# A decoder layer on one core: the operands of all large products laid to the same place modulo 512 bytes

## The chip, the core and the metric

The kernel runs on one core of one Trainium2 chip. The core has five engines that run side by side: TensorE (PE, matrix products; its loading of the stationary operand is shown apart as PEld), VectorE (DVE), ScalarE (ACT), GpSimd (POOL) and SyncE (SP), whose queue issues most of the DMA transfers. SBUF is the working memory, 128 partitions wide; a tile is a stretch of bytes at the same address in each partition. PSUM takes the results of the products. The metric is the device time of one execution in microseconds (us), lower being better.

## The reference

One layer works on 256 positions of width 2048 (all sizes float32):

```
h    = RMSNorm(x);  qkv = h @ W_in
8 heads: stick-breaking attention;  8 heads: rotary + dilated sliding-window attention
x    = x + RMSNorm(concat(RMSNorm per head) @ W_out)
h    = RMSNorm(x);  u = causal depthwise conv (width 3) of h @ W_up   (W_up: 2048 x 11008)
f    = gelu(gate half of u) * (value half of u)
x    = x + RMSNorm(f @ W_down)                                       (W_down: 5504 x 2048)
```

Nearly all of the arithmetic is in the four products with W_in, W_out, W_up and W_down.

## The kernel before

**Precision.** Each large product is made of three: both operands are split into a high part (rounded to the float32r format that TensorE takes) and a low remainder, and high x high, low x high and high x low are summed in PSUM. ScalarE makes the high part of a weight (`high`, line 85), VectorE the low part (`low`, line 90).

**Weights.** They are loaded from DRAM in pieces of 128 x 1024 float32 into `raw` (5 buffers), and their parts go to `wh` and `wl` (4 buffers each), all in the pool `wpool`. `ahead` loads two chunks ahead and splits one chunk ahead of use.

**The large products**, each a stationary operand of 128 x 128 that is loaded anew for each matmul, and a moving operand that streams past it:

- `mm_stationary` (lines 96 to 104): results `mmqk` (queries and keys) and `mmu` (up projection). The weight is stationary, the activation `hT2` moves. In groups of 16: eight matmuls of 512 columns (line 101, the high part of the weight against high and low of the activation at once) and eight of 256 (line 104, low against high). `mm_stationary_late` (line 110) does the first two chunks of the up projection in another order, with 256 columns each.
- `mm_moving` (lines 132 to 149): results `mmv` (values) and `mmo` (output projection). The activation is stationary, `hT2` for `mmv` and the pair `mix` for `mmo`; the weight moves, 512 columns (lines 143, 144, 147).
- `Down.multiply` (lines 621 to 623): result `p`, the down projection; `yt` and `yp` (the activation) are stationary, the weight moves, 512 columns, and 256 for the last 24.

Small products of the attention (lines 340 to 419) stand between those of the first part. One of them is the pair of lines 387 and 388, 384 columns, in which `sph` and `spl` move past `tri`.

**Order.** The chunks of all the products run one after the other in one list; at each chunk the kernel issues its loads, splits and matmuls, and then lets the attention heads advance by a step. The order within an engine is the order of the program, fixed by hand in the passages where `pinned` is set. No wait is written by hand: the framework puts in those that the data and the buffers need.

**Where the tiles lie.** A pool lays its tiles one behind the other, in the order in which they first appear, each rounded up to 32 bytes; the pools follow each other. `cpool` begins at byte 384 of a partition. A float32 tile row of 128 takes 512 bytes, and every slice that the products take of a tile begins a multiple of 512 bytes from the tile's start. What decides the place modulo 512 are thus the tiles whose size is no multiple of 512: `par` (1568 bytes), `rstd1` (8, rounded to 32), `gpre` (64) and the pool `small` (2496 in all).

`along_rows` (line 305) turns a value per position into a row that all partitions hold: VectorE scales the identity by the values (line 310) and TensorE multiplies it by a tile of ones (line 311). It is used twice.

Of the kernel before, what the change touches and what calls it, by code (L numbers as in the profile page):

```python
# [9 lines left out]
F32 = mybir.dt.float32  # L10
F32R = mybir.dt.float32r
BF16 = mybir.dt.bfloat16
AF = mybir.ActivationFunctionType
ALU = mybir.AluOpType
PSUM = bass.MemoryType.PSUM

P = 128
D = 2048
S = 256
KT = D // P  # L20
# [31 lines left out]
def layer_kernel(ctx: ExitStack, tc: tile.TileContext, a, out: bass.AP):  # L52
    nc = tc.nc
    V, A, T, G = nc.vector, nc.scalar, nc.tensor, nc.gpsimd

    cpool = ctx.enter_context(tc.tile_pool(name="cpool", bufs=1))
    wpool = ctx.enter_context(tc.tile_pool(name="wpool", bufs=3))
    small = ctx.enter_context(tc.tile_pool(name="small", bufs=4))
# [139 lines left out]


    A.preload_act_table_set("natural_log_exp_and_others")  # L200
    par = cpool.tile([P, P_END], F32, name="par")
    ident = cpool.tile([P, P], F32, name="ident")
    hT2 = cpool.tile([P, KT, 2, S], F32R, tag="hT", name="hT")
    hT = [hT2[:, :, i, :] for i in range(2)]

    phA = tc.tile_pool(name="phA", bufs=2)
    apool = phA.__enter__()
    cst = apool.tile([P, C_END - P], F32, name="cst", bufs=1)
    gpre = apool.tile([P, KT], F32, name="gpre", bufs=1)
    x1 = apool.tile([P, 2, D], F32, name="x1", bufs=1)  # L210
    x1_kept = nc.dram_tensor("x1_kept", (S, D), F32, kind="Internal").ap()

# [77 lines left out]
    between[10] = (cst, a["cst"][:, 0:C_ID])  # L290
    between[11] = (par, a["par"])

    negones = apool.tile([P, P], F32, name="negones", bufs=1)
    G.memset(negones, -1.0)
    ones = cpool.tile([P, P], F32, name="ones")
    G.memset(ones, 1.0)
    tri = apool.tile([P, P], F32R, name="tri", bufs=1)
    idb = apool.tile([P, P], BF16, name="idb", bufs=1)
    mskb = apool.tile([P, P], BF16, name="mskb", bufs=1)
    rB = apool.tile([P, 2, S], F32, name="rB", bufs=1)  # L300
    cosR = apool.tile([P, 2, S], F32, name="cosR", bufs=1)
    sinR = apool.tile([P, 2, S], F32, name="sinR", bufs=1)
    rstd1 = cpool.tile([P, 2], F32, name="rstd1")

    def along_rows(r, name):

        ps = ps_at.tile([P, S], F32, tag="at", name=name)
        for t in range(2):
            dg = small.tile([P, P], F32, tag="diag", name="diag", bufs=1)
            V.tensor_scalar(dg, ident, r[t], None, op0=ALU.mult)  # L310
            T.matmul(ps[:, t * P:(t + 1) * P], ones, dg, start=True, stop=True)
        return ps

    def first_norm():

        V.tensor_copy(tri, cst[:, C_TRI:C_TRI + P])
        G.tensor_copy(idb, ident)
        G.tensor_copy(mskb, cst[:, C_MSK:C_MSK + P])
        ss = small.tile([P, 2], F32, tag="ssx", name="ssx", bufs=1)
        for t in range(2):  # L320
            A.activation(gbc, x1[:, t, :], AF.Square, accum_out=ss[:, t:t + 1])
        v0 = small.tile([P, 2], F32, tag="vx", name="vx", bufs=1)
        V.tensor_scalar(v0, ss, 1.0 / D, EPS, op0=ALU.mult, op1=ALU.add)
        V.tensor_copy(rstd1, rstd_of(v0, 2))
        rps = along_rows((rstd1[:, 0:1], rstd1[:, 1:2]), "rps")
        V.tensor_scalar(rB[:, 0, :], rps, SCALE, None, op0=ALU.mult)
        V.tensor_copy(rB[:, 1, :], rps)
        for s in range(2):
            V.tensor_tensor(cosR[:, s, :], cst[:, C_COS:C_COS + S], rB[:, s, :], op=ALU.mult)
            V.tensor_tensor(sinR[:, s, :], cst[:, C_SIN:C_SIN + S], rB[:, s, :], op=ALU.mult)  # L330
# [129 lines left out]
    def second_norm():  # L460

        rs = [sq.newton(*sq.mean(t)) for t in range(2)]
        r2B = cpool.tile([P, S], F32, name="r2B")
        V.tensor_scalar(r2B, along_rows(rs, "r2ps"), -0.5, None, op0=ALU.mult)
        return r2B
# [273 lines left out]
    for i, (kind, p, s, _, w) in enumerate(chunks):  # L739
        parts = ahead(i, 0 if (kind, p, s) == ("out", 3, 3) else SPLITS)  # L740
        if kind == "v":
            if s == 0:
                pool, tag = (ps_at, "at") if p == 1 else (ps_mm, "mm")
# [26 lines left out]
        elif kind == "qk":  # L770
            ps = ps_mm.tile([P, 2, S], F32, tag="mm", name="mmqk")
# [8 lines left out]
        elif kind == "out":  # L780
# [14 lines left out]
            else:  # L795
                pinned[0] = True
                up0 = []
                r = [None, None]
# [97 lines left out]
        else:  # L896
            ps = ps_mm.tile([P, 2, S], F32, tag="mm", name="mmu")
# [96 lines left out]
```

## Time and profile before

| what | value |
|---|---|
| median of 3 runs | 1117.11 us (1116.38 to 1117.14) |
| the profiled execution, its time | 1117.05 us |
| its span, first to last instruction | 1115.3 us |
| granted TensorE clock | 0.998 |
| TensorE busy / weight loads | 1103.5 us / 942.1 us |
| VectorE / ScalarE / GpSimd busy | 879.4 / 661.3 / 5.7 us |
| matmuls | 5855 |
| moved by DMA | 257.79 MB, mean 231 GB/s |

The profile is one execution, recorded by the hardware. A line number such as L101 is that of the kernel; `mmu<-hT,wl` names the tile written and the tiles read. In a row of groups stand the number of instructions after the x, then the busy time in us and the mean duration of one in ns, then the idle time before them. In a row by tile stand the shortest, median and longest duration in ns, and when the first and the last began. In a row of the stretches stand the bounds, the length, and then the busy time of PE, PEld, DVE, ACT and POOL with the number of their instructions, the granted clock, the DMA share and GB/s. A matmul's recorded duration reaches beyond the start of the next one, since matmuls are pipelined.

### The profile page before, as it was taken

To read this page: it belongs to the slowest core of one execution; us is meant where nothing else is said; L and a number is where in the kernel's file an instruction comes from. 1 tells how busy PE (TensorE), PEld (TensorE's weight loads), DVE (VectorE), ACT (ScalarE), POOL (GpSimd) and SP (SyncE) were. 2 spreads that over 40 slices of the span, in tenths; PEclk is the share of its full clock that TensorE was granted. 3 is DMA by queue.
4 is the path that set the end of the run, shared out by engine and by line. 5 is a ranking of instruction groups with operands and counts; after the bars stand their busy time and mean duration, and the time that the engine had idled before them with its cause. 6 is when DMAs were issued, how large, how long until landed. Compare 5 with 4: busy or idle time off the path is not lost.

```text
span 1115.3 us, 16308 instructions
## 1 busy us (share of the span) xinstructions
PE 1103.5 (99%) x5855; PEld 942.1 (84%) x5855; DVE 879.4 (79%) x1371; ACT 661.3 (59%) x1046; POOL 5.7 (1%) x13
## 2 busy tenths in 40 slices
PE   9999999999999999999999999999999999999997
PEld 6888888888888888888888888888888888888885
DVE  6577776777776589878888878888878898889887
ACT  6656665655654476655555555555555566666564
POOL 0000000000000000000000000000000000000001
PEclk9999999999999999999999999999999999999999
DMA  9977777877879856555555555555555577767775
GB/s 322 360 261 270 254 252 273 295 255 274 274 258 321 274 199 212 190 189 190 187 189 184 189 186 186 186 188 188 189 188 188 174 250 242 251 217 252 240 244 208
DMA packets 75393, 257.79 MB, mean 231 GB/s; under 512 B 8496, under 2 KB 9520, under 8 KB 74544
## 3 DMA queue, kind: packets, MB, share of 16 engines
q1 hardware_dynamic: 74880, 256.22, 68.9%
q8 instruction: 46, 0.75, 0.3%
q10 hardware_dynamic: 432, 0.53, 0.1%
q14 instruction: 35, 0.29, 0.1%
HBM read 238.89 MB, written 17.83 MB: 230 GB/s over the span
## 4 chain that ended last, share of the span: by engine, by line
PE 98%; DMA 0%; DVE 0%; ACT 0%; issue 0%; SPq 0%; DVEq 0%; ACTq 0%
PE mmu L101 28%; PE mmu L104 14%; PE mmqk L101 11%; PE p L621 7%; PE p L623 7%; PE p L622 6%; PE mmqk L104 5%; PE mmv L144 3%; PE mmv L147 3%; PE mmv L143 3%; PE mmo L143 3%; PE mmo L144 3%; PE mmo L147 3%; PE mmu L110 1%; DMA raw<-in_w_v 0%; PE po L341 0%
## 5 line engine op out<-in xcount | busy, mean ns | idle before, releaser
L88 ACT CAST wh<-raw 128x1024 fp32r<-128x1024 f32 (+1 forms) x408 | 414.8, 1024 | 355.9 <-PE mmu L101 190.1
L93 DVE TENSOR_TENSOR wl<-raw,wh 128x1024 fp32r<-128x1024 f32 (+1 forms) x408 | 482.4, 1189 | 165.4 <-ACT wh L88 160.7
L101 PE MATMUL mmu<-hT,wh 128*128 128x512 f32 x1344 | 340.5, 395 | 0.0
L101 PEld LDWEIGHTS mmu<-hT,wh 128*128 128x128 f32 x1344 | 240.8, 188 | 44.6
L104 PEld LDWEIGHTS mmu<-hT,wl 128*128 128x128 f32 x1344 | 184.1, 188 | 15.3
L104 PE MATMUL mmu<-hT,wl 128*128 128x256 f32 x1344 | 187.3, 281 | 0.0
L101 PE MATMUL mmqk<-hT,wh 128*128 128x512 f32 x512 | 133.0, 401 | 0.0
L101 PEld LDWEIGHTS mmqk<-hT,wh 128*128 128x128 f32 x512 | 92.0, 188 | 17.2
L104 PEld LDWEIGHTS mmqk<-hT,wl 128*128 128x128 f32 x512 | 69.9, 188 | 5.8
L621 PE MATMUL p<-wh,yp 128*128 128x512 f32 x182 | 71.7, 394 | 0.0
L623 PE MATMUL p<-wl,yp 128*128 128x512 f32 x182 | 71.5, 393 | 0.0
L104 PE MATMUL mmqk<-hT,wl 128*128 128x256 f32 x512 | 71.1, 281 | 0.0
L622 PE MATMUL p<-wh,yp 128*128 128x512 f32 x182 | 70.7, 388 | 0.0
L621 PE MATMUL p<-wh,yt 128*128 128x512 f32 (+1 forms) x140 | 54.2, 387 | 0.0
L623 PE MATMUL p<-wl,yt 128*128 128x512 f32 (+1 forms) x140 | 53.8, 386 | 0.0
L622 PE MATMUL p<-wh,yt 128*128 128x512 f32 (+1 forms) x140 | 53.5, 382 | 0.0
L494 ACT ACTIVATE cv<-u,par 128x256 f32<-128x256 f32 x86 | 51.5, 599 | 2.5 <-DVE u L492 2.3
L143 PE MATMUL mmv<-wh,hT 128*128 128x512 f32 x128 | 51.4, 403 | 0.3 <-ACT hT L225 0.3
L144 PE MATMUL mmv<-wh,hT 128*128 128x512 f32 x128 | 50.7, 396 | 0.5 <-DVE hT L272 0.2
L143 PE MATMUL mmo<-wh,mix 128*128 128x512 f32 x128 | 50.4, 394 | 0.0
L88 ACT CAST wh<-room 128x1024 fp32r<-128x1024 f32 x26 | 27.3, 1048 | 38.7 <-PE p L622 36.4
L144 PE MATMUL mmo<-wh,mix 128*128 128x512 f32 x128 | 49.9, 390 | 0.0
(179 smaller groups left out, 1221.8 us busy)
## 6 DMA issues: line engine op xcount, KB each, us to landing
raw<-in_w_up SPq DMA_DIRECT2D x172, 512.0 KB, 4.3
raw<-in_w_qk SPq DMA_DIRECT2D x64, 512.0 KB, 4.9
raw<-in_w_dn SPq DMA_DIRECT2D x60, 512.0 KB, 4.5
raw<-in_w_o SPq DMA_DIRECT2D x32, 512.0 KB, 5.1
raw<-in_w_v SPq DMA_DIRECT2D x28, 512.0 KB, 5.2
t<-in_w_dn SPq DMA_DIRECT2D x26, 512.0 KB, 5.6
t_kept<-t SPq DMA_DIRECT2D x26, 512.0 KB, 3.9
raw<-t_kept SPq DMA_DIRECT2D x26, 512.0 KB, 4.4
```

The lines of the kernel that those rows point to most:

```text
L88: pin(A.copy(wh, raw))
L93: pin(V.tensor_tensor(wl, raw, wh.bitcast(F32), op=ALU.subtract))
L101: T.matmul(ps, wh[:, j * P:(j + 1) * P], h[:, k, :, :], start=(k == 0), stop=False, skip_group_check=True)
L104: T.matmul(ps[:, 0, :], wl[:, j * P:(j + 1) * P], h[:, k, 0, :], start=False, stop=(k == KT - 1), skip_group_check=True)
L110: T.matmul(ps[:, part, :], parts[k // 8][low][:, k % 8 * P:(k % 8 + 1) * P], h[:, k, part, :], skip_group_check=True, **kw)
L143: T.matmul(ps[t], hi[:, k, tc_], ws, start=(first and i == 0 and j == 0), stop=False)
L144: T.matmul(ps[t], lo[:, k, tc_], ws, start=False, stop=False)
L147: T.matmul(ps[t], hi[:, k, tc_], wl[:, j * 512:(j + 1) * 512], start=False, stop=(last and i == len(parts) - 1 and j == n - 1))
L494: A.activation(cv, u, AF.Identity, scale=cw(2), bias=par[:, P_CB + f:P_CB + f + 1])
L621: T.matmul(ps, yh, wh[:, cs], start=key not in self.begun, stop=False)
L622: T.matmul(ps, yl, wh[:, cs], start=False, stop=False)
L623: T.matmul(ps, yh, wl[:, cs], start=False, stop=self.left[key] == 0)
```

## The change

Nothing is computed anew; tiles lie elsewhere.

```diff
+    hT2 = cpool.tile([P, KT, 2, S], F32R, tag="hT", name="hT")
+    ident = cpool.tile([P, P], F32, name="ident")
+    negones = cpool.tile([P, P], F32, name="negones")
     par = cpool.tile([P, P_END], F32, name="par")
-    ident = cpool.tile([P, P], F32, name="ident")
-    hT2 = cpool.tile([P, KT, 2, S], F32R, tag="hT", name="hT")
...
-    gpre = apool.tile([P, KT], F32, name="gpre", bufs=1)
+    gpre = small.tile([P, KT], F32, name="gpre", bufs=1)
...
-    negones = apool.tile([P, P], F32, name="negones", bufs=1)
     G.memset(negones, -1.0)
-    ones = cpool.tile([P, P], F32, name="ones")
-    G.memset(ones, 1.0)
...
-    rstd1 = cpool.tile([P, 2], F32, name="rstd1")
+    rstd1 = cpool.tile([P, 2], F32, name="rstd1", padded_shape=[P, 2 + 112])
...
-            V.tensor_scalar(dg, ident, r[t], None, op0=ALU.mult)
-            T.matmul(ps[:, t * P:(t + 1) * P], ones, dg, start=True, stop=True)
+            V.tensor_scalar(dg, ident, r[t], -1.0, op0=ALU.mult, op1=ALU.mult)
+            T.matmul(ps[:, t * P:(t + 1) * P], negones, dg, start=True, stop=True)
```

The tile of ones goes; the tile of minus ones, which the attention uses anyway, serves in its place, and the identity is scaled by minus the values. `hT2` moves ahead of `par`, `rstd1` is padded to 114 elements, and `gpre` moves into `small`. The places that follow, from the sizes:

| tile | before: byte, modulo 512 | after: byte, modulo 512 |
|---|---|---|
| `hT2` | 2464, 416 | 384, 384 |
| `raw`, `wh`, `wl` (first of each) | 36800, 57280, 73664; all 448 | 37248, 57728, 74112; all 384 |
| `mix` (two) | 113600, 129984; both 448 | 114048, 130432; both 384 |
| `yt` (two), `yp` (two) | 92544, 109952, 127360, 173952; all 384 | 93056, 110464, 127872, 174464; all 384 |
| `tri`; `sph`, `spl` | all 448 | all 384 |

After, by the sums: 384 + 32768 (`hT2`) + 512 (`ident`) + 512 (`negones`) + 1568 (`par`) + 480 (`rstd1`, 456 rounded up) + 1024 (`r2B`) = 37248, where `wpool` begins; it is 104 x 512 bytes long. `small` has 2496 + 64 = 2560 = 5 x 512 bytes, so what follows begins at 384 modulo 512 again.

So the pairs (moving operand, stationary operand) are, modulo 512, before: `mmqk` and `mmu` 416 and 448; `mmv` 448 and 416; `mmo` 448 and 448; `p` 448 and 384. After, all are 384 and 384.

## The prediction

> **What bounds the kernel now.** I read the page first, then the waits of TensorE, the busy time by stretch, and last the starts of single matmuls.
>
> ```profile
> PE 1103.5 (99%) x5855; PEld 942.1 (84%) x5855; DVE 879.4 (79%) x1371; ACT 661.3 (59%) x1046; POOL 5.7 (1%) x13
> ...
> PEclk9999999999999999999999999999999999999999
> ...
> PE 98%; DMA 0%; DVE 0%; ACT 0%; issue 0%; SPq 0%; DVEq 0%; ACTq 0%
> ```
>
> TensorE is busy for 99% of the span at full granted clock, and the chain that ended last runs 98% on it. Its longest waits for others, from the view of waits, are these:
>
> ```profile
> PE pth L821 <- DVE x L813: 1.2, 1, 1.2
> PE mmv L143 <- ACT hT L225: 0.3, 1, 0.3
> ```
>
> The stretches (stage of the v products, up projection, down projection) show what stands behind TensorE:
>
> ```profile
> 28.00:56.00 28.00, 28.00 (x126) 22.69 (x125) 14.11 (x22) 18.20 (x24) 0.81 (x2) 1.00 0.96 360
> 448.00:868.00 420.00, 420.00 (x2392) 366.84 (x2391) 347.09 (x565) 244.41 (x364) 0.00 (x0) 1.00 0.58 187
> 896.00:1092.00 196.00, 195.99 (x856) 160.49 (x856) 173.72 (x191) 125.42 (x141) 0.00 (x0) 1.00 0.76 241
> ```
>
> So the end is set by how fast matmuls follow each other. A busy share says nothing about that; I need the spacing from start to start. In the up projection the chain of waits, in order of time, gives it for whole groups (start, length, what):
>
> ```profile
> 440.88 1.86 PE mmu L101 x8
> 442.74 0.95 PE mmu L104 x8
> ...
> 476.50 0.95 PE mmu L104 x8
> 477.45 1.86 PE mmu L101 x8
> ```
>
> There are 13 groups of 8 + 8 from 440.88 to 477.45: 36.57 / 13 = 2.813 us a group. The durations of single matmuls, by tile within quiet stretches (min/median/max in ns), split it:
>
> ```profile
> L104 PE MATMUL mmu<-hT,wl x1198: 277/281/288, 448.2 to 868.0; 128*128 128x256 f32 x200
> L101 PE MATMUL mmu<-hT,wh x1194: 392/395/397, 447.7 to 867.2; 128*128 128x512 f32 x199
> ```
>
> A duration is the spacing plus a tail that overlaps the next matmul. With 395 - 281 = 114 ns between the two and 2813 / 8 = 351.6 ns for one of each, the 512-column step takes 232.8 ns and the 256-column step 118.8; the tail is 162 ns in both. From here, **spacing = duration - 162**.
>
> **What the address does, as the trace of before shows it.** The addresses in front (section on the change) give four combinations of where the two operands of a product begin, modulo 512 bytes. In `mmv` and `mmo` the code is the same (lines 143 to 147), the shape is the same, the streamed weights are the same buffers; the stationary operand alone differs, `hT` (416 against 448 of the weights) or `mix` (448, equal):
>
> ```profile
> L147 PE MATMUL mmv<-wl,hT x20: 393/395/397, 28.6 to 41.4; 128*128 128x512 f32 x20
> L147 PE MATMUL mmo<-wl,mix x84: 389/389/389, 335.8 to 391.8; 128*128 128x512 f32 x84
> L623 PE MATMUL p<-wl,yp x170: 392/392/392, 899.8 to 1090.0; 128*128 128x512 f32 x170
> L621 PE MATMUL p<-wh,yp x169: 394/394/394, 900.0 to 1089.5; 128*128 128x512 f32 x169
> L622 PE MATMUL p<-wh,yp x169: 388/388/388, 900.2 to 1089.8; 128*128 128x512 f32 x169
> ```
>
> The equal pair is the quickest and takes one value for all 84; the unequal ones spread over 388 to 397. Starts confirm it. `mmo` (12 steps, 2.72 us, 226.7 ns each):
>
> ```profile
> 340.35 0.39 PE L143 MATMUL mmo<-wh,mix 128*128 128x512 f32 x1
> 340.58 0.39 PE L144 MATMUL mmo<-wh,mix 128*128 128x512 f32 x1
> ...
> 343.07 0.39 PE L143 MATMUL mmo<-wh,mix 128*128 128x512 f32 x1
> ```
>
> `mmv` (12 steps, 2.80 us, 233.3 ns each):
>
> ```profile
> 29.04 0.40 PE L143 MATMUL mmv<-wh,hT 128*128 128x512 f32 x1
> ...
> 31.84 0.40 PE L143 MATMUL mmv<-wh,hT 128*128 128x512 f32 x1
> ```
>
> And the down products (64 bytes apart; 15 steps, 3.43 us, 228.7 ns each):
>
> ```profile
> 1000.03 0.39 PE L623 MATMUL p<-wl,yp 128*128 128x512 f32 x1
> ...
> 1003.46 0.39 PE L623 MATMUL p<-wl,yt 128*128 128x512 f32 x1
> ```
>
> My reading, which no row proves, is that the weight load of the next product and the stream of the running one hinder each other in SBUF, least where both begin at the same place.
>
> The Trainium skill speaks against it. On the page "TensorE: Matmul & The Clock Gate", section "Step-by-step: what each phase is for", it says that "Loading the next tile's weights doesn't steal SBUF read bandwidth from the running matmul", and "SBUF — State Buffer", section "Who interferes with whom", has TensorE wait on nobody. By that rule the place of an operand is worth nothing and the time stays at 1117; by the rows it is worth 6 to 7 ns a step. The trace speaks against the rule as far as it reaches here, and I go by the rows.
>
> **The change part by part.** Afterwards every operand of `mmqk`, `mmu`, `mmv`, `mmo` and `p` begins at 384 modulo 512 (sizes added up in front), so the layout does what it says.
>
> *512-column steps of the stationary products* (L101, 1344 + 512 = 1856): 232.8 to 226.7, gain 6.1 ns each, **11.3 us**. If they came only to the 228.7 of the down products it would be 7.6.
>
> *256-column steps* (L104, 1856): no quiet row has this width with equal places, so I bound it. The rows, three as groups (busy us, mean ns) and one by tile (min/median/max ns):
>
> ```profile
> L362 PE MATMUL pt<-ident,on 128*128 128x128 f32 x32 | 6.1, 272 | 0.0
> L388 PE MATMUL z<-spl,tri 128*128 128x384 f32 x8 | 2.7, 336 | 0.0
> L623 PE MATMUL p<-wl,yt 128*128 128x256 f32 x8 | 2.2, 279 | 0.0
> ```
>
> ```profile
> L110 PE MATMUL mmu<-hT,wh x64: 274/282/388, 401.1 to 413.6; 128*128 128x256 f32 x64
> ```
>
> Below: a 128-column step, which has a weight load to wait for and little else, takes 272 - 162 = 110; the quickest 256-column step of all (274) takes 112. Above: `z<-spl,tri` has equal places (448 and 448) and 384 columns and takes 174; going on by the same 52.7 ns per 128 columns from 226.7 gives 121.3. Between: the down products have both widths at the same two places, 228.7 and 279 - 162 = 117, so 111.7 less for half the columns; in the up projection the step is 114. From 226.7 that makes 115.0 or 112.7. I take 115.5, the down products being nearest to equal, with a little for the case above: 118.8 - 115.5 = 3.3 ns, 1856 times, **6.1 us**. Ends: 110 gives 16.3 us, 121.3 gives a loss of 4.6.
>
> *`mmv`* (3 x 128 = 384 steps): 6.6 ns each, 2.5 us. Half of them lie in the first 56 us, where DMA is at 0.96 and may not deliver sooner, so I count the other half and half of these: **1.9 us**. *Down products* (966 steps, nearly all of 512 columns): 228.7 - 226.7 = 2.0 each, **1.9 us**. *`mmo`*: equal before and after, nothing. *The late products of the first pair* (L110, 96 steps) at 3.3: **0.3 us**.
>
> *One tile of ones less*: its MEMSET ran on POOL, 1% busy, beside the first loads. The minus sign is a second operation inside four VectorE instructions that exist already:
>
> ```profile
> L310 DVE TENSOR_SCALAR diag<-ident,rstd x2: 279/282/285, 53.4 to 57.5; 128x128 f32<-128x128 f32 x2
> L310 DVE TENSOR_SCALAR diag<-ident,rs x2: 276/281/286, 420.6 to 422.6; 128x128 f32<-128x128 f32 x2
> ```
>
> I take nothing; if each took twice as long and nothing covered it, 4 x 0.28 = 1.1 us. No DMA, wait or queue position is moved; buffers keep their number.
>
> Sum: 11.3 + 6.1 + 1.9 + 1.9 + 0.3 = 21.5 us. The profiled execution took 1117.05 us (span 1115.3), the median of the runs is 1117.11, so they can stand for each other: 1117.05 - 21.5 = **1095.5**.
>
> **The rivals.**
>
> *A fixed price per step.* If what is left of the hindrance is paid once per weight load, whatever the width, the 256-column steps go to 121.3 as above: 1095.5 + 6.1 + 4.6 = **1106.2**. For it: `z<-spl,tri`. Against: in both pairs of rows at unequal places the price shrinks with the width.
>
> *256-column steps fall to the weight load*, 110 ns: 1095.5 - 10.2 = **1085.3**. For it: single steps already reach 112. Against: `mmo` too keeps a price at equal places.
>
> *Another bound takes over.* VectorE is at 347 of 420 us in the up projection and 174 of 196 in the down; TensorE going 2.5% quicker puts it at 85% and 89%, still below. Only in the first 300 us, where loads run at up to 0.96, could the gain be given back: without `mmqk` (512 of the 1856 steps) and `mmv` 12.6 + 1.9 + 0.3 = 14.8 stays: **1102.3**.
>
> *The place is not the cause*, and by this rival the change doesn't do what it is for (it is the skill's rule). `mix` also differs from `hT2` in being two tiles 16 KB apart, where `hT2` interleaves high and low halves every 1 KB. Then nothing moves: **1117**. Against: `yt` and `yp` are separate tiles too and pay 2 ns.
>
> *Slower: an equal start is the worst start for the 256-column steps.* There the next weight load begins as soon as the last ends, and if both reads collide at both ends of each step, at 6.6 ns a collision, 118.8 becomes 132: 13.2 x 1856 = 24.5 us lost against 11.3 + 1.9 + 1.9 gained: **1126.5**. It decides from 118.8 + 15.1 / 1.856 = 127 ns, a duration of 289. Against: that is above the slowest (288) of the 1198 steps today, and `mmo` shows no such thing.
>
> **How the numbers follow.** Forecast 0.58; fixed price 0.16; weight load as the floor 0.10; another bound 0.05; place not the cause 0.06; slower 0.05. Runs of before lie within 0.07%; I take 0.2%, 2.2 us, as what can be told from no change. Faster holds the first four, 0.89; same 0.06; slower 0.05. The range goes from just under the floor case (1084) to past the fixed price (1108).
>
> **What would show it.** The median duration of L101 `mmu` falls from 395 to 389 with hardly any spread; L104 from 281 to 277 or 278 (272 in the floor case, 283 with the fixed price, 289 and more if slower); `mmv` 389; the three rows of `p` all 389 in place of 388 to 394; `mmo` stays at 389. A group of 8 + 8 takes 2.74 us in place of 2.813. I am wrong if those durations stay where they are, or if they fall and TensorE begins to show waits for VectorE or loads.

## The result and the profile after

The changed kernel takes 1108.84 us (median of four runs, 1108.83 to 1109.59); the kernel before took 1116.77 beside it. The ratio is 0.9931, 95% interval 0.9913 to 0.9948: faster by about 8 us, where 21.5 were forecast. 1108.8 lies just above the upper end of the range.

The page after, from the engines and the chain that ended last:

```profile
PE 1095.9 (99%) x5855; PEld 942.7 (85%) x5855; DVE 879.1 (79%) x1371; ACT 661.3 (60%) x1046; POOL 5.3 (0%) x12
...
PE 97%; DMA 1%; DVE 0%; ACT 0%; SPq 0%; issue 0%; DVEq 0%; ACTq 0%
```

The stretch of the up projection after (bounds, length, busy time of PE, PEld, DVE, ACT, POOL, clock, DMA share, GB/s):

```profile
448.00:868.00 420.00, 420.00 (x2410) 369.73 (x2409) 348.83 (x568) 246.24 (x366) 0.00 (x0) 1.00 0.59 189
```

The bound has not moved: TensorE is as busy as before, VectorE does 348.8 us of work in 420. So the missing gain was not handed to another engine; the matmuls did not close up as far as forecast. Where they did and where they didn't is in the durations by tile (min/median/max in ns; a spacing is the duration less 162):

```profile
L147 PE MATMUL mmv<-wl,hT x22: 389/389/389, 28.1 to 42.0; 128*128 128x512 f32 x22
L147 PE MATMUL mmo<-wl,mix x80: 389/389/390, 335.7 to 388.9; 128*128 128x512 f32 x80
L101 PE MATMUL mmu<-hT,wh x1202: 389/392/398, 447.7 to 867.9; 128*128 128x512 f32 x172
L104 PE MATMUL mmu<-hT,wl x1208: 277/283/284, 447.9 to 867.8; 128*128 128x256 f32 x173
L104 PEld LDWEIGHTS mmu<-hT,wl x1207: 187/192/193, 447.9 to 867.7; 128*128 128x128 f32 x173
L620 PE MATMUL p<-wh,yp x161: 389/389/390, 899.9 to 1076.7; 128*128 128x512 f32 x161
L621 PE MATMUL p<-wh,yp x161: 389/389/389, 900.1 to 1076.9; 128*128 128x512 f32 x161
L622 PE MATMUL p<-wl,yp x161: 389/389/390, 900.3 to 1077.1; 128*128 128x512 f32 x161
```

`mmv` and all three rows of `p` now stand at 389 like `mmo`, as forecast. The stationary products don't: the 512-column steps spread from 389 to 398, and the 256-column steps became slower (median 283 after 281) though more even. The chain in order of time after:

```profile
440.68 1.84 PE mmu L101 x8
442.52 0.95 PE mmu L104 x8
...
474.20 1.84 PE mmu L101 x8
```

That is 12 groups in 33.52 us, 2.793 us a group after 2.813. Taken from the start of each matmul to the start of the next and summed by product over both traces, in us:

| steps | before | after | difference | forecast |
|---|---|---|---|---|
| `mmqk`, `mmu`, 512 columns | 435.1 | 430.4 | -4.7 | -11.3 |
| `mmqk`, `mmu`, 256 columns (with L110) | 232.9 | 233.4 | +0.5 | -6.4 |
| `mmv` | 91.9 | 90.1 | -1.9 | -1.9 |
| `p` | 218.6 | 216.6 | -2.0 | -1.9 |
| `mmo` | 87.8 | 87.8 | 0.0 | 0 |
| all others | 39.1 | 39.0 | -0.1 | 0 |

Within a group of the changed kernel the eight wide steps (512 columns) start 233, 236, 228, 233, 231, 227, 227 and 227 ns after each other, and the narrow ones (256 columns) that follow 113, 119 and then 120 (medians over the up projection). That is what the experiments set out from: equal places bring 227, but only after five steps, and bring the narrow steps to 120.

### The profile page after: what moved, and what is told of

It is laid out like the page before. It is cut to its first block, busy times and chain, and to the rows that moved or that the text cites. A ratio compares the mean times of both kernels' runs of the same rounds, so it can differ in the third digit from the quotient of the medians.

```text
span 1107.0 us, 16307 instructions
## 1 busy us (share of the span) xinstructions
PE 1095.9 (99%) x5855; PEld 942.7 (85%) x5855; DVE 879.1 (79%) x1371; ACT 661.3 (60%) x1046; POOL 5.3 (0%) x12
## 4 chain that ended last, share of the span: by engine, by line
PE 97%; DMA 1%; DVE 0%; ACT 0%; SPq 0%; issue 0%; DVEq 0%; ACTq 0%
PE mmu L101 28%; PE mmu L104 14%; PE mmqk L101 11%; PE p L622 7%; PE p L620 7%; PE p L621 7%; PE mmqk L104 6%; PE mmo L147 3%; PE mmo L143 3%; PE mmo L144 3%; PE mmv L147 2%; PE mmv L143 2%; PE mmv L144 2%; PE mmu L110 1%; DMA mg<-in_xT 1%; DMA raw<-in_w_v 0%
## 5 line engine op out<-in xcount | busy, mean ns | idle before, releaser
L88 ACT CAST wh<-raw 128x1024 fp32r<-128x1024 f32 (+1 forms) x408 | 414.6, 1024 | 348.3 <-PE mmu L101 186.6
L101 PE MATMUL mmu<-hT,wh 128*128 128x512 f32 x1344 | 336.8, 392 | 0.0
L622 PE MATMUL p<-wl,yp 128*128 128x512 f32 x182 | 70.9, 390 | 0.0
L622 PE MATMUL p<-wl,yt 128*128 128x512 f32 (+1 forms) x140 | 53.4, 383 | 0.0
```

Source lines behind the costliest of these rows:

```text
L88: pin(A.copy(wh, raw))
L101: T.matmul(ps, wh[:, j * P:(j + 1) * P], h[:, k, :, :], start=(k == 0), stop=False, skip_group_check=True)
L622: T.matmul(ps, yh, wl[:, cs], start=False, stop=self.left[key] == 0)
```

## The experiments

Three theories: (1) the spacing is made within TensorE, by the distance between both operands' places and by what ran before; (2) it comes from the other engines and DMA in SBUF; (3) the prediction's: equal places, and nothing else, give 227 and about 115.

**A map of distances** (`map`). The layer is replaced by stationary products alone:

```diff
+    def wide(ps, k, d, **kw):
+        T.matmul(ps, W(wh, k), h[:, d + 512 * k:d + 512 * k + 512], skip_group_check=True, **kw)
 
+    def narrow(ps, k, d, **kw):
+        T.matmul(ps[:, 0:S], W(wl, k), h[:, d + 512 * k:d + 512 * k + S], skip_group_check=True, **kw)
```

> No part of the layer is computed here: copies of the inputs serve as operands, and the output is not the layer's. TensorE runs stationary products alone, with nearly nothing else on the chip, at 16 distances between the place of the moving operand and that of the stationary one modulo 512 bytes: letter a is 0 bytes apart, b 32, and so on to p, 480. For each letter there are 32 steps of 512 columns (wide), 32 of 256 (narrow) and 6 groups of 8 wide and 8 narrow (group). Theory 1, place and history: the spacing hangs on the distance and, after a change of width, on what went before; wide_a has a median duration of 389 (spacing 227), narrow_a 282 (120), and in group_a the wide steps spread over 389 to 398 as in the changed kernel, while wide_p (32 bytes behind, the place before) is at 393 to 396. Theory 2, the neighbours: the spacing above the plain streaming time comes from the other engines and DMA in SBUF; then all letters are alike and quicker than in the layer. Theory 3, place alone, as in the prediction: group_a has its wide steps at 389 like wide_a.

Rows of groups in the map (busy us, mean ns of one), the mixed groups at 0, 64, 96 and 480 bytes and the steps of one width at 256 and 480:

```profile
L77 PE MATMUL wide_i<-h,wh 128*128 128x512 f32 x32 | 7.4, 389 | 0.0
L77 PE MATMUL wide_p<-h,wh 128*128 128x512 f32 x32 | 7.6, 395 | 0.0
...
L80 PE MATMUL narrow_i<-h,wl 128*128 128x256 f32 x32 | 4.0, 283 | 0.0
L80 PE MATMUL narrow_p<-h,wl 128*128 128x256 f32 x32 | 4.0, 281 | 0.0
...
L77 PE MATMUL group_a<-h,wh 128*128 128x512 f32 x48 | 12.0, 392 | 0.0
L77 PE MATMUL group_c<-h,wh 128*128 128x512 f32 x48 | 12.0, 391 | 0.0
L77 PE MATMUL group_d<-h,wh 128*128 128x512 f32 x48 | 12.2, 395 | 0.0
L77 PE MATMUL group_p<-h,wh 128*128 128x512 f32 x48 | 12.2, 395 | 0.0
...
L80 PE MATMUL group_a<-h,wl 128*128 128x256 f32 x48 | 6.7, 282 | 0.0
L80 PE MATMUL group_c<-h,wl 128*128 128x256 f32 x48 | 6.5, 278 | 0.0
L80 PE MATMUL group_d<-h,wl 128*128 128x256 f32 x48 | 6.7, 282 | 0.0
L80 PE MATMUL group_p<-h,wl 128*128 128x256 f32 x48 | 6.7, 281 | 0.0
```

From the starts in this trace (one execution), the settled spacing of each width alone and the time of a group of 8 + 8:

| distance, bytes | wide, ns | narrow, ns | group, us |
|---|---|---|---|
| 0 | 226.7 | 120.0 | 2.793 |
| 32 | 233.3 | 116.7 | 2.800 |
| 64 | 228.9 | 117.8 | 2.756 |
| 96 | 233.4 | 120.0 | 2.827 |
| 128 | 232.3 | 119.9 | 2.810 |
| 160 | 234.3 | 118.5 | 2.807 |
| 192 | 233.4 | 117.8 | 2.773 |
| 224 | 233.4 | 118.4 | 2.813 |

From 256 on the table repeats, so what counts is the distance modulo 256 (for letter a, whose wide steps hold the first load and the cold start, the value is that of i, 256 bytes). With nothing else running, the group at 0 takes what it takes in the changed kernel (2.793 in both) and the one at 480, which is 224 modulo 256, what it takes in the kernel before (2.813 in both). Theory 2 falls: the spacing is there with TensorE alone at work. Theory 3 falls with `group_a` at 392, not 389. And equal places are not the best: 64 bytes apart, a group is 37 ns shorter. The map shifts the moving operand alone; that the distance counts, and not the place of the moving operand by itself, is seen in the layer: `mmo` stands at 389 with both operands at 448 and with both at 384.

**Does each step follow its own distance, and does order count** (`map2`). The same operands, groups with separate distances for wide and narrow, and other orders:

```diff
+    def groups(dw, dn, n, size=8):
+        return [(what, (size * g + j) % 16, d) for g in range(n) for what, d in ((wide, dw), (narrow, dn)) for j in range(size)]
```

> As in the first map, no part of the layer is computed: stationary products alone on copies of the inputs. Two letters: group_ac has the wide steps 0 bytes apart and the narrow ones 64 (a to h: 0 to 224 in steps of 32). sixteen_ has 16 wide and 16 narrow steps in turn, turns_ one and one, half_ distances 16 bytes above the letter's, word_ 4, 8, 68 and 72 bytes. If a step's spacing followed from its own distance alone, group_ac would have its wide steps as in group_aa (230 ns) and its narrow ones as in group_cc (114 to 116), 2.76 us a group or less. If what went before counts, group_ac is not the sum of the two, and sixteen_a has the second half of its wide steps at 227, so that a wide and a narrow step together take 347.5 ns against 349.2 in group_aa. Distances that are no multiple of 32: no theory; if SBUF is read in lines of 16 bytes or more, word_w and word_x are like group_aa.

By tile in this map (min/median/max):

```profile
L77 PE MATMUL group_ac<-h,wh x32: 389/392/398, 49.2 to 59.2; 128*128 128x512 f32 x32
L80 PE MATMUL group_ac<-h,wl x32: 279/280/283, 51.1 to 60.3; 128*128 128x256 f32 x32
L77 PE MATMUL sixteen_a<-h,wh x48: 389/389/397, 744.3 to 758.9; 128*128 128x512 f32 x48
L77 PE MATMUL turns_a<-h,wh x32: 395/398/403, 761.0 to 771.9; 128*128 128x512 f32 x32
```

The narrow steps of `group_ac` have the distance of `group_cc` and not its time: `group_ac` takes 2.786 us, while the wide half of `group_aa` (8 x 230.1 ns) and the narrow half of `group_cc` (8 x 115.7) would make 2.766; its narrow steps take 118.1 ns on average. What went before counts. `turns_a`, where the width changes at every step, has wide steps at 398 at the very distance where a run of them has 389; in `sixteen_a` the second eight are at 227. Of all 64 pairs of distances the best is `group_cc`, 2.756 (the worst, 2.833); distances between the multiples of 32 gave 2.786 to 2.866, and operands 4 or 8 bytes apart (`word_w` 2.866, `word_x` 2.826) are not like operands at equal places (2.793).

**64 bytes apart in the layer** (`ht64`):

```diff
+    apart = cpool.tile([P, 16], F32, name="apart")
+    V.memset(apart, 0.0)
     hT2 = cpool.tile([P, KT, 2, S], F32R, tag="hT", name="hT")
...
-    rstd1 = cpool.tile([P, 2], F32, name="rstd1", padded_shape=[P, 2 + 112])
+    rstd1 = cpool.tile([P, 2], F32, name="rstd1", padded_shape=[P, 2 + 96])
```

> The changed kernel with hT2 alone moved up by 64 bytes, so that the moving operand of mmqk and mmu begins 64 bytes behind the weights; mmo and p stay equal, mmv gets minus 64. Theory 1 (the spacing is made in TensorE by distance and history, as in the map): a group of 8 + 8 goes from 2.794 to 2.756 us, 232 times 38 ns, 8.8 us less; mmv goes from 227 to 233, 384 steps, up to 2.5 us more; 1108.8 - 6.3 = 1102.5. Theory 3 (equal is best, as predicted): slower than 1108.8, back towards 1114. If other engines take over as the bound: not below 1106.

Measured 1103.37 us, ratio to the kernel before 0.9878 (0.9863 to 0.9892). By tile:

```profile
L147 PE MATMUL mmv<-wl,hT x21: 393/398/398, 27.8 to 41.8; 128*128 128x512 f32 x21
L101 PE MATMUL mmu<-hT,wh x1220: 388/392/394, 447.6 to 867.3; 128*128 128x512 f32 x175
L104 PE MATMUL mmu<-hT,wl x1220: 276/279/283, 448.5 to 867.9; 128*128 128x256 f32 x175
```

Against the changed kernel the stationary products need 7.5 us less (1.6 in the wide steps, 5.9 in the narrow) and `mmv`, now 192 bytes apart modulo 256, gives back 2.3, where theory 1 had 8.8 less and up to 2.5 more: its time holds to within a microsecond. Theory 3 (slower) falls, and so does a bound by other engines (not below 1106). `mmv` leaves the 389 it has in the changed kernel although its moving operand, the weights, lies where it lay. This is the quickest of all versions of the layer here.

**Sixteen wide steps, then sixteen narrow** (`sixteen`):

```diff
         for i, (wh, wl) in enumerate(parts):
             for j in range(8):
                 k = 8 * i + j
                 T.matmul(ps, wh[:, j * P:(j + 1) * P], h[:, k, :, :], start=(k == 0), stop=False, skip_group_check=True)
+        for i, (wh, wl) in enumerate(parts):
             for j in range(8):
```

> The changed kernel with the order of the stationary products turned: 16 wide steps of a chunk, then its 16 narrow ones, in place of 8 and 8 twice; places as in the changed kernel. Theory 1: only the first 8 wide steps after narrow ones pay the extra 29 ns, so half of it goes, 116 times 29 = 3.4 us, less 0.9 for the quick first narrow step that is had half as often: 1106.3. Theory 3 (spacing by address alone): 1108.8 as before.

Measured 1106.19, ratio 0.9902 (0.9885 to 0.9918). The median of the wide steps is now the settled 389:

```profile
L101 PE MATMUL mmu<-hT,wh x1206: 389/389/398, 447.6 to 866.3; 128*128 128x512 f32 x173
L105 PE MATMUL mmu<-hT,wl x1213: 277/283/283, 449.0 to 867.9; 128*128 128x256 f32 x174
```

So in the changed kernel part of the loss is the settling after each change of width.

**The worst distance** (`ht96`): as `ht64`, with a tile of 24 elements and `2 + 88`.

> As ht64, with hT2 moved up by 96 bytes in place of 64: a distance between hT2 and the weights that no kernel so far had, and the worst of the map's equal-letter groups (d, 2.827 us a group). Theory 1: 232 groups at 33 ns more than in the changed kernel, 7.7 us, and mmv at 160 bytes (letter f, 234 ns against 227), up to 2.8 us: 1108.8 + 10.5 = 1119.3, slower than the kernel before (1117.0). Theory 3, equal or not being all that counts: like the kernel before in its stationary products and mmv, about 1115.

Measured 1118.52, ratio 1.0014 (1.0004 to 1.0023): slower than the kernel before, by 0.14%, although `p` keeps its gain and `mmo` its time. Theory 1 had 1119.3, theory 3 1115. A group takes, from the chain of this kernel:

```profile
442.36 1.87 PE mmu L101 x8
444.23 0.96 PE mmu L104 x8
...
476.28 1.87 PE mmu L101 x8
```

12 groups in 33.92 us, 2.827, as in the map.

**The tile of ones alone** (`ones_only`), on the kernel before:

```diff
-    ones = cpool.tile([P, P], F32, name="ones")
-    G.memset(ones, 1.0)
...
+            V.tensor_scalar(dg, ident, r[t], -1.0, op0=ALU.mult, op1=ALU.mult)
+            T.matmul(ps[:, t * P:(t + 1) * P], negones, dg, start=True, stop=True)
```

> The kernel before with one part of the change alone: no tile of ones, minus ones in its place and the second operation in the four VectorE instructions; every place modulo 512 as before (the tile taken out is 512 bytes long). Prediction and theory 1: 1117, within 0.2%, since nothing on TensorE's path changes. If this part had a share in the result: below 1115.

Measured 1117.26, ratio 1.0001 (0.9992 to 1.0010). This part is worth nothing that can be told within 0.1%; the change's effect comes from the places.

**What in TensorE costs the time** (`map3`). Fewer columns of weights per load, and narrower streams, at 0, 64 and 224 bytes:

```diff
+    def step(ps, k, d, cols, width, **kw):
+        T.matmul(ps[0:cols, 0:width], W(wh, k)[:, 0:cols], h[:, d + 512 * k:d + 512 * k + width], skip_group_check=True, **kw)
```

> No part of the layer is computed: stationary products alone, at distances a (0), c (64) and h (224 bytes; the place of the kernel before is the same modulo 256). load_: 512 columns, with 128 (full), 96 (most), 64 (half) or 32 (little) columns of weights loaded for each step. width_: 512 columns down to 128 (r to x, 64 less each), full weights. size_: two or four wide steps and as many narrow ones in turn. If the stream and the load of the next weights hinder each other, the spacing of 512 columns falls with the columns loaded, from 233 (h), 229 (c) and 227 (a) towards one value for all three, near 216, which is 512 columns at the 0.417 ns that a further column costs plus a few ns. If the extra time is the stream's own, by where it begins, it stays at 227 to 233 whatever is loaded. A fixed price per step gives width_ of letter a a straight line of 0.41 to 0.42 ns a column from 227 at 512 to 120 at 256; a price in proportion gives 113 there.

Rows of groups (mean ns of one in the last but one place):

```profile
L77 PE MATMUL load_full_a<-h,wh 128*128 128x512 f32 x32 | 7.4, 389 | 0.0
L77 PE MATMUL load_little_a<-h,wh 128*32 128x512 f32 x32 | 7.6, 394 | 0.0
L77 PE MATMUL load_full_h<-h,wh 128*128 128x512 f32 x32 | 7.6, 396 | 0.0
L77 PE MATMUL load_most_h<-h,wh 128*96 128x512 f32 x32 | 7.5, 390 | 0.0
L77 PE MATMUL load_little_h<-h,wh 128*32 128x512 f32 x32 | 7.8, 401 | 0.0
...
L77 PE MATMUL load_full_c<-h,wh 128*128 128x512 f32 x32 | 7.6, 397 | 0.0
L77 PE MATMUL width_r_c<-h,wh 128*128 128x512 f32 x32 | 7.5, 392 | 0.0
...
L77 PE MATMUL width_s_a<-h,wh 128*128 128x448 f32 x32 | 6.6, 365 | 0.0
L77 PE MATMUL width_t_a<-h,wh 128*128 128x384 f32 x32 | 5.7, 335 | 0.0
L77 PE MATMUL width_t_h<-h,wh 128*128 128x384 f32 x32 | 5.7, 336 | 0.0
L77 PE MATMUL width_v_a<-h,wh 128*128 128x256 f32 x32 | 4.0, 283 | 0.0
```

A quarter of the weights to load does not bring the step towards 216: the settled spacing goes from 226.7 to 231.6 at distance 0 and from 233.3 to 240.0 at 224. Nor does it stay where it was whatever is loaded: at 224 it is 228.9 with 96 columns of weights and 231.6 with 64, at 64 bytes 228.4 with 64 columns. So neither expectation came true. The plain picture, that the load's reads stand in the stream's way for as long as they last, falls, and no other is shown in its place. The rows for c show how much history weighs: the same 32 instructions at the same distance settled at 233.3 in one place of the program and at 228.7 in another.

Of the widths at distance 0, four lie on a straight line, 226.7 (512), 173.3 (384), 146.7 (320) and 120.0 ns (256): 0.417 ns a column and **13.3 ns a step**. The line is not a law for every width: 448 columns take 202.5, 2.5 ns above it, and 192 and 128 columns both take about 111.6. At 384 and 320 columns the distance makes no difference (173.3 and 146.6 to 146.7 at all three).

## Why the prediction was wrong

**What held.** TensorE's spacing was the bound and stayed it. The place of the operands moves it: with TensorE alone at work, 512 columns take 226.7 or 233.3 ns by distance. The Trainium skill says on the page "TensorE: Matmul & The Clock Gate", section "Step-by-step: what each phase is for", that loading the next weights takes no SBUF read bandwidth from the running matmul, and on "SBUF — State Buffer", section "Who interferes with whom", that TensorE waits on nobody. What the prediction drew from it for the rival, that the place is worth nothing, is refuted by the map and by `p`, whose three rows all came to 389. Whether the two reads hinder each other is not shown by any run here.

The terms for `p`, `mmo` and the tile of ones came out within 0.2 us each. The term for `mmv` did too, but by luck in its halves: of the 1.9 us, 1.0 came in the first 56 us, where the prediction counted on 0.6 because of the loads, and 0.8 later, where it counted on 1.3. From the 65th to the 192nd step, begun between 21 and 52 us, the full 6.7 ns a step were gained, although the DMA share was 0.96 or more there.

**The step that failed most: "256-column steps", 115.5 ns.** It stands at 119.1 on average (120 once settled) and the term at +0.5 in place of -6.4 us with the late products. I took half the columns to carry about half the price, from rows at unequal places. At equal places 256 columns pay as much as 512: 13.3 ns a step on top of 0.417 ns a column (`map3`). The 115.5 belongs to another distance: the narrow steps of `ht64` come to 115.7, at 64 bytes, which is the distance of the down products from whose rows the number was mostly taken.

The rival "a fixed price per step" was right for the narrow steps (121.3 forecast, 120 found); it had a chance of 0.16. Its 1106.2 is still 2.6 us short, since it kept 226.7 for the wide steps. And it was right partly by luck: the row on which it stood, `z<-spl,tri` (174 ns at 384 columns), shows nothing of equal places, because at 384 columns `map3` has 173.3 at 0, 64 and 224 bytes alike. The same extrapolation at 224 bytes would give 113.4 for 256 columns, where 118.2 was found.

**The second: "512-column steps of the stationary products", 226.7 ns.** It is 230.1 over the group, the term -4.7 in place of -11.3 us. I carried over the 389 of `mmo`, whose 84 quiet steps are all of one width. After eight narrow steps the wide ones need five steps to come to 227; `sixteen` pays this half as often and is 2.65 us quicker. The trace of before held the hint. The three rows of `p` have one distance and stood at 394, 388 and 392, each at one value throughout, so distance alone could not be the whole law. The prediction read these rows as "The equal pair is the quickest", which the 388 of L622, below the 389 of `mmo`, contradicts.

With both errors the sum is 21.5 - 6.9 - 6.6 = 8.0 us, which is the measured gain. The rival "slower" did not come true by its mechanism anywhere: it had narrow steps of 132 ns, and in `ht96`, the one version of the layer that is slower than the kernel before, they take 119.9 and the wide ones 233.4. (One slip changed nothing: VectorE at 174 of 196 us would go to 91%, not 89%, if the down products became 2.5% quicker.) My reading that the weight load and the stream hinder each other is not shown. That the spacing goes by distance modulo 256 and by history, with TensorE alone at work, is shown; what inside makes it stays open.

## What to carry to other kernels

Where matmuls run back to back, compare their spacing between products of the same shape; a difference of a few nanoseconds can come from where the operands begin, and moving a tile adds no work. Don't carry a spacing over to another sequence: map the distances with the very sequence of widths that the kernel has, since the best distance for the wide steps alone (0 bytes) was not the best for the mix (64). Where no row has the width and the distance that a change brings about, as here with 256 columns at equal places, rows of another width or another distance bound it poorly: a small kernel that runs that step in its sequence does better. The map's 2.793 us a group is what the changed kernel takes, and its figures at 64 and 96 bytes gave the times of `ht64` and `ht96` to within a microsecond.

## What the hardware showed beyond expectation

- The distance counts modulo 256 bytes, not 512: the settled spacings repeat 256 bytes on to within 0.1 ns (wide 233.3 at 32 and at 288 bytes).
- The order of widths is worth as much as the place: at distance 0 the wide step takes 226.7 ns in a run, 230.1 in groups of eight, 236.0 when widths take turns.
- Two settled states at one distance: 228.7 and 233.3 ns at 64 bytes for the same instructions.
- At equal places the narrow steps' weight loads are recorded longer too, with a median of 192 ns after 188 in the kernel before.
